# Low halves of the input projection's weights: stored in the second group of tokens instead of the first

## The chip, the cores and the metric

The kernel runs on one core of a Trainium2 chip. The metric is the device time of one execution in microseconds (us); lower is better. A core has five engines that run side by side, each working through its own list of instructions in order: TensorE (PE: matrix products; its weight loads are shown apart as PEld), VectorE (DVE), ScalarE (ACT), GpSimd (POOL) and SyncE (SP, which here issues nearly all DMA transfers). Engines wait for one another through semaphores. SBUF is the on-chip memory, PSUM the accumulators behind TensorE, and DRAM the chip's main memory.

## The reference

One decoder layer over 2048 tokens of width 1024, all in float32:

```
a = rmsnorm(x);  u = a @ W_in                      # 1024 -> 2560 columns
conv half:  glu = val * sigmoid(gate); causal depthwise conv of width 31; layernorm; silu
attention half: 8 heads of 64, stick-breaking attention
                A[t,s] = sigmoid(z_ts) * prod_{s<j<t} (1 - sigmoid(z_tj)), s < t;  then a head-wise rmsnorm
y = concat(conv, attn) @ W_out;  h = x + rmsnorm(y)
f = swiglu(rmsnorm(h)) with 2816 hidden columns;  out = h + rmsnorm(f)
```

## The kernel before

**Products in two halves.** TensorE multiplies in a reduced float32 format. To keep full precision, every operand X is split into a high half H, which is X rounded to that format by ScalarE, and a low half L = X - H. Each product is then three matmuls: L·H', H·H' and H·L'. For weights, ScalarE makes H (L554) and GpSimd makes L (L558); for activations, VectorE makes L.

**Groups.** The tokens are four groups of 512. The input projection (`inproj`, plan entry "in") runs once for each group. It goes through 20 weight blocks of 128 x 1024 (four each of gate, val, q, k, v), each of 512 KB in float32, and each takes 24 matmuls (`dense`; the lines L600, L602, L604 of the profile). The output projection (`outproj`, 8 tiles of weights) also runs for each group, and the first feed-forward products (`c11`, 22 tiles) for two of the groups.

**Weights.** `load_w` brings one weight tile. `Weights.next` calls it two blocks ahead of use; the tiles `raw`, `wH` and `wL` rotate through 2, 3 and 3 buffers. It loads the raw weights (L553) and makes H (L554). The first time that a tile is used it makes L (L558) and stores it to DRAM (L560) under the key of its source and number in the dictionary `kept`; at each later use it loads L from there (L556) and GpSimd does nothing. So of the 80 input-projection blocks, the 20 of group 0 are made and stored, and the 60 of groups 1 to 3 are loaded.

**What runs beside it.** The list `PLAN` sets the main stages. Three side streams are drawn along by the position in it: the attention (`attn_s`), the taps of the convolution (`taps_s`, on VectorE, L826) and sums of feed-forward weights (`sums_s`, on GpSimd, L1201). In the attention, a block of scores is turned into products by a scan on VectorE: for blocks on the diagonal L916 with the constant mask `lower` and the tile `om`, both in SBUF; for the others L918, one of whose operands is in PSUM. The result is transposed by TensorE (L936), split (ScalarE L592 makes TH, VectorE L593 makes TL) and multiplied with the values (L941, L942).

**Order.** All instructions up to the end of the mixing part (about 1420 us) are collected in a `Graph`. A list scheduler (`arrange`) with a cost for each kind of instruction, for transfers and for hops between engines simulates them, tries 13 orders, and keeps the shortest. `in_order` then pins each engine's order to it. The scheduler treats engines as independent of each other apart from data and buffers. SP's queue is ordered by it too; a DMA whose data or buffer isn't ready holds up the DMAs behind it. After that the rest of the feed-forward part (`five` and the down projection) runs in an order written out in the code.

Of the kernel before, what the change touches and what calls it, by code (L numbers as in the profile page):

```python
# [10 lines left out]
F32 = mybir.dt.float32  # L11
# [8 lines left out]
P = 128  # L20
S = 2048
D = 1024
# [459 lines left out]
def layer_kernel(ctx: ExitStack, tc: tile.TileContext, x, xT, g_pre_mix, w_in, conv_w, conv_b, ln_g, ln_b,  # L482
                 attn_g, w_out, g_post_mix, g_pre_ffn, w_gate, w_up, w_down, g_post_ffn, out):
    nc = tc.nc
    cp = ctx.enter_context(tc.tile_pool(name="consts", bufs=1))
    dp = ctx.enter_context(tc.tile_pool(name="scratch", bufs=1, space=DRAM))
# [57 lines left out]
    kept = {}  # L544

    def load_w(w):

        src, n = w
        H = wp.tile([P, D], F32R, tag="wH", name="wH", bufs=3)
        L = wp.tile([P, D], F32R, tag="wL", name="wL", bufs=3)  # L550
        key = id(src), n
        raw = wp.tile([P, D], F32, tag="raw", name="raw")
        nc.sync.dma_start(raw, src[n])  # L553
        nc.scalar.activation(H, raw, AF.Copy)  # L554
        if key in kept:
            nc.sync.dma_start(L.bitcast(F32), kept[key])  # L556
            return H, L
        nc.gpsimd.tensor_tensor(L, raw, H.bitcast(F32), ALU.subtract)  # L558
        kept[key] = dp.tile([P, D], F32, name=f"wL_{len(kept)}")
        nc.sync.dma_start(kept[key], L.bitcast(F32))  # L560
        return H, L

    def half_w(w):
# [10 lines left out]
    class Weights:  # L574


        def __init__(self, srcs, ahead=2, load=load_w):
            self.srcs = list(srcs)
            self.load = load
            self.tiles = []  # L580
            self.n = 0
            self.ahead = ahead
# [1222 lines left out]
```

## Time and profile before

| | us |
|---|---|
| Median of 3 runs | 2428.36 |
| Lowest and highest | 2428.14, 2428.55 |
| Profiled execution, its own time | 2429.93 |
| Span of the profiled execution | 2428.1 |

The span is the time from the first to the last instruction of the profiled execution. "Busy" is the time in which an engine executes at least one instruction. An idle stretch is put down to the event that ended it. In the views below a line such as L558 is a line of the kernel, "x20" a count, and "x<-y" a tile written from y. The DMA figures of the page are 656.67 MB moved in all, 270 GB/s on average. Among the queues, SP's carries 77.3% of the time of 16 DMA engines.

Of the low halves, the trace has 50 made and stored (20 of the input projection, 8 of the output projection, 22 of `c11`) and 106 loaded (60, 24 and 22).

### The profile page before, as it was taken

What the parts mean: (1) busy time and instruction counts of PE and PEld (TensorE: products, weight loads), DVE (VectorE), ACT (ScalarE), POOL (GpSimd) and SP (SyncE); (2) the same over time, 40 slices, a digit from 0 to 9 for tenths busy, and PEclk for the clock granted to TensorE, in tenths of its full rate; (3) what the DMA queues carried; (4) which work ended last, traced back from release to release, by engine and by line L of the source; (5) the groups of instructions that cost most, each with busy time, mean ns of one, the idle gap of its engine ahead of it and who ended that gap; (6) DMA issues with size and microseconds to landing.
All of it is one profiled execution on the core that took longest, in us unless ns stands there. A gap on an engine that the chain in (4) does not pass through costs nothing. (4 is left out here: it accounts for less than half of the span.)

```text
span 2428.1 us, 33643 instructions
## 1 busy us (share of the span) xinstructions
PE 2353.6 (97%) x11156; PEld 1929.4 (79%) x11156; DVE 1766.3 (73%) x2177; ACT 1163.8 (48%) x2078; POOL 1196.0 (49%) x994
## 2 busy tenths in 40 slices
PE   7999999999999999999999998999999999999998
PEld 5778888788888878887888877777888888887886
DVE  6897899999997799847832357667666664556557
ACT  4346555574555455455564553333232235454443
POOL 5462336422424333428700057755766665467656
PEclk9999999999999999999999999999999999999999
DMA  9888876998688899987897769878888877668765
GB/s 315 266 263 313 259 248 216 308 314 266 223 300 310 264 321 341 314 290 257 266 341 244 272 227 335 310 257 277 295 286 267 271 253 257 196 191 280 236 191 178
DMA packets 283790, 656.67 MB, mean 270 GB/s; under 512 B 34912, under 2 KB 35424, under 8 KB 283616
## 3 DMA queue, kind: packets, MB, share of 16 engines
q1 hardware_dynamic: 267776, 625.68, 77.3%
q10 hardware_dynamic: 15840, 28.84, 3.1%
q8 instruction: 88, 1.44, 0.2%
q14 instruction: 86, 0.70, 0.1%
HBM read 460.40 MB, written 193.99 MB: 270 GB/s over the span
## 5 line engine op out<-in xcount | busy, mean ns | idle before, releaser
L826 DVE SCALAR_TENSOR_TENSOR cv<-glu,cw,cv 128x512 f32<-128x512 f32 x464 | 346.9, 748 | 6.2
L1411 POOL TENSOR_TENSOR wL<-raw,wH 128x512 fp32r<-128x512 f32 x176 | 254.8, 1470 | 194.5 <-ACT wH L1410 163.1
L1642 DVE TENSOR_TENSOR xL__20078<-t__20080,xH__20077 128x512 fp32r<-128x512 f32 x154 | 200.4, 1306 | 159.9 <-ACT xH__20077 L1641 159.8
L1640 POOL TENSOR_TENSOR xL__20076<-t__20079,xH__20075 128x512 fp32r<-128x512 f32 x154 | 212.7, 1388 | 153.6 <-ACT xH__20075 L1639 145.4
L593 DVE TENSOR_TENSOR TL<-at,TH 128x512 fp32r<-128x512 f32 (+1 forms) x320 | 189.5, 601 | 127.7 <-ACT TH L592 117.3
L600 PE MATMUL inps<-xH,wL 128*128 128x512 f32 x640 | 259.4, 406 | 9.9 <-ACT sg L770 8.8
L604 PE MATMUL inps<-xL,wH 128*128 128x512 f32 x640 | 255.7, 401 | 0.6 <-DVE xL L740 0.6
L602 PE MATMUL inps<-xH,wH 128*128 128x512 f32 x640 | 256.3, 401 | 0.0
L1117 PE MATMUL dps<-xL__20076,xH__20077 128*128 128x512 f32 x616 | 240.1, 390 | 2.8 <-POOL xL__20076 L1640 2.8
L1117 PE MATMUL dps<-xH__20075,xL__20078 128*128 128x512 f32 x616 | 240.1, 390 | 2.5 <-DVE xL__20078 L1642 2.1
L1117 PE MATMUL dps<-xH__20075,xH__20077 128*128 128x512 f32 x616 | 239.8, 389 | 0.0
L554 ACT ACTIVATE wH<-raw 128x1024 fp32r<-128x1024 f32 x156 | 165.4, 1061 | 139.9 <-PE inps L604 62.9
L592 ACT ACTIVATE TH<-at 128x512 fp32r<-128x512 f32 (+1 forms) x320 | 168.8, 537 | 130.2 <-PE at L936 113.7
L913 ACT ACTIVATE om<-z 128x512 f32<-128x512 f32 (+2 forms) x320 | 168.8, 542 | 89.3 <-PE z L911 87.8
L1639 ACT ACTIVATE xH__20075<-t__20079 128x512 fp32r<-128x512 f32 x154 | 97.3, 632 | 217.2 <-POOL xL__20076 L1640 121.2
L558 POOL TENSOR_TENSOR wL<-raw,wH 128x1024 fp32r<-128x1024 f32 x50 | 123.1, 2467 | 155.9 <-ACT wH L554 119.3
L936 PE MATMUL at<-idr,om 128*128 128x128 f32 x1088 | 185.4, 273 | 7.2 <-DVE TL L593 2.7
L1410 ACT ACTIVATE wH<-raw 128x512 fp32r<-128x512 f32 x176 | 101.2, 623 | 167.7 <-PE b L1117 49.8
L936 PEld LDWEIGHTS at<-idr,om 128*128 128x128 f32 x1088 | 136.8, 140 | 48.0 <-DVE TL L593 6.3
L1201 POOL TENSOR_TENSOR sum<-sum 128x512 f32<-128x512 f32 x88 | 124.6, 1416 | 100.2 <-DMA sum<-in_w_up_dram 40.3
L918 DVE TENSOR_TENSOR_SCAN om<-om,z 128x512 f32<-128x512 f32 x124 | 156.8, 1271 | 8.5 <-ACT om L913 8.2
L600 PEld LDWEIGHTS inps<-xH,wL 128*128 128x128 f32 x640 | 121.7, 190 | 34.5 <-ACT sg L770 5.8
(296 smaller groups left out, 6103.9 us busy)
## 6 DMA issues: line engine op xcount, KB each, us to landing
wL<-wL SPq DMA_DIRECT2D x156, 512.0 KB, 5.3
raw<-in_w_in_dram SPq DMA_DIRECT2D x80, 512.0 KB, 5.8
t__20080<-u SPq DMA_DIRECT2D x154, 256.0 KB, 2.8
c<-c ACTq DMA_DIRECT2D x88, 256.0 KB, 5.3
t__20079<-wd SPq DMA_DIRECT2D x88, 256.0 KB, 2.9
K<-kd SPq DMA_DIRECT2D x80, 256.0 KB, 4.9
V<-vd SPq DMA_DIRECT2D x80, 256.0 KB, 5.0
u<-accf SPq DMA_DIRECT2D x22, 768.0 KB, 4.6
```

What stands on the lines that cost most here:

```text
L592: nc.scalar.activation(H, ps, AF.Copy)
L593: nc.vector.tensor_tensor(L, ps, H.bitcast(F32), ALU.subtract)
L600: nc.tensor.matmul(ps, WL[:, kc], aH[t](k), start=k == 0, stop=False)
L602: nc.tensor.matmul(ps, WH[:, kc], aH[t](k), start=False, stop=False)
L604: nc.tensor.matmul(ps, WH[:, kc], aL[t](k), start=False, stop=k == KT - 1)
L826: nc.vector.scalar_tensor_tensor(to, gl[c][:, k:k + G], cw[:, c, k:k + 1], a, ALU.mult, ALU.add)
L913: nc.scalar.activation(om[:, 0:w], z[:, 0:w], AF.Sigmoid, scale=-0.125)
L936: nc.tensor.transpose(pt[:, j * P:(j + 1) * P], u["A"][j][:, b * P:(b + 1) * P], id32)
L1117: return nc.tensor.matmul(ps, a, b, skip_group_check=True, **flags)
L1411: nc.gpsimd.tensor_tensor(l, t, f32(h), sub)
L1640: nc.gpsimd.tensor_tensor(WL, w, f32(WH), sub)
L1642: nc.vector.tensor_tensor(UL, t, f32(UH), sub)
```

## The change

For weights of the input projection (`src is w_in`) the first use makes the low half and returns without storing it; the key gets an empty tuple. The second use finds the empty tuple, makes the low half once more, allocates the DRAM tile and stores it. The third and fourth uses load it. Weights of other matrices are made and stored at the first use, as before. The value in the dictionary becomes a tuple with one tile. The name of a new DRAM tile is still taken from the number of keys in the dictionary, which doesn't grow between the second uses of the 20 blocks.

```diff
-        if key in kept:
-            nc.sync.dma_start(L.bitcast(F32), kept[key])
+        if kept.get(key):
+            nc.sync.dma_start(L.bitcast(F32), kept[key][0])
             return H, L
         nc.gpsimd.tensor_tensor(L, raw, H.bitcast(F32), ALU.subtract)
-        kept[key] = dp.tile([P, D], F32, name=f"wL_{len(kept)}")
-        nc.sync.dma_start(kept[key], L.bitcast(F32))
+        if src is w_in and key not in kept:
+            kept[key] = ()
+            return H, L
+        kept[key] = dp.tile([P, D], F32, name=f"wL_{len(kept)}"),
+        nc.sync.dma_start(kept[key][0], L.bitcast(F32))
         return H, L
```

Counted over the kernel: 20 more subtractions on GpSimd (70 for 50), 20 fewer loads of low halves (86 for 106), and as many stores (50), 20 of them later.

## The prediction

> **What bounds the kernel now.** I read the page first: the engine totals and the busy tenths in 40 slices.
>
> ```profile
> span 2428.1 us, 33643 instructions
> PE 2353.6 (97%) x11156; PEld 1929.4 (79%) x11156; DVE 1766.3 (73%) x2177; ACT 1163.8 (48%) x2078; POOL 1196.0 (49%) x994
> ...
> PE   7999999999999999999999998999999999999998
> ...
> DVE  6897899999997799847832357667666664556557
> ...
> DMA  9888876998688899987897769878888877668765
> ```
>
> TensorE is busy for 97% of the span, so the time can move only by what TensorE waits, and all its idle time is 2428.1 - 2353.6 = 74.5 us. The change touches no matmul. Behind TensorE the slices show VectorE nearly full through the first third, and DMA at eight or nine tenths but not full.
>
> Next I cut the span where the low halves are made and loaded: those of group 0 are made before 157 us (the view of L558 below), and group 1's stretch goes from there to about 360 us. This is the view by stretches; its columns are PE, PEld, DVE, ACT and POOL busy, the clock, the DMA share and GB/s.
>
> ```profile
> 0.00:157.00 157.00, 134.55 (x627) 108.62 (x628) 125.15 (x171) 65.54 (x112) 91.02 (x88) 0.98 0.89 282
> 157.00:360.00 203.00, 199.57 (x1060) 165.41 (x1058) 179.21 (x266) 119.56 (x222) 65.81 (x77) 1.00 0.84 273
> ...
> 157.00:200.00 43.00, 42.11 (x225) 35.38 (x224) 40.48 (x64) 26.39 (x51) 13.01 (x14) 1.00 0.89 301
> 200.00:280.00 80.00, 79.12 (x426) 65.38 (x424) 59.72 (x88) 49.38 (x92) 25.06 (x38) 1.00 0.90 296
> 280.00:360.00 80.00, 78.34 (x414) 64.66 (x412) 79.01 (x116) 43.80 (x80) 27.73 (x26) 1.00 0.76 235
> ```
>
> TensorE is idle 157 - 134.55 = 22.4 us in group 0 and 203 - 199.57 = 3.4 us in group 1. GpSimd is 58% busy in group 0 (91.02 of 157) and 32% in group 1 (65.81 of 203). VectorE has 20.3 us to spare between 200 and 280 us, and almost none at 280 to 360 us (79.01 of 80). Then I asked what TensorE waited for, first up to 157 us, then from 157 to 360 us (total us, times, longest).
>
> ```profile
> PE tps L610 <- DVE xrow L686: 11.0, 4, 7.3
> PE inps L600 <- ACT sg L770: 5.9, 2, 4.7
> PE at L936 <- DVE om L916: 2.1, 2, 1.3
> PE o L942 <- DVE TL L593: 1.5, 1, 1.5
> PE at L936 <- DVE TL L593: 1.1, 1, 1.1
> ...
> PE at L936 <- ACT ma L976: 0.9, 1, 0.9
> PE cps L853 <- DVE acc L847: 0.6, 1, 0.6
> PE z L910 <- DVE om L918: 0.5, 1, 0.5
> PE inps L600 <- DVE glu L775: 0.5, 1, 0.5
> ```
>
> No row names a DMA or a weight tile. In both groups TensorE waits for VectorE and ScalarE, and for weights never. In group 1 only some 2.5 us is there to be won at all.
>
> **The change part by part.** In group 0, `load_w` still makes the low half on GpSimd (L558) but no longer stores it. In group 1 it makes the low half again and stores it then. Groups 2 and 3 load it as now. So 20 stores move from group 0 to group 1, 20 loads of group 1 go, and 20 GpSimd subtractions come into group 1. The view of L558 by stretches and the list of DMA issues give the sizes:
>
> ```profile
> 0.00:157.00 157.00, 50.16 (x20) 0.98 0.89 282
> 157.00:360.00 203.00, 4.90 (x3) 1.00 0.84 273
> ...
> L558 POOL TENSOR_TENSOR wL<-raw,wH x50: 2344/2404/3321, 11.4 to 1036.9; 128x1024 fp32r<-128x1024 f32 x50
> ...
> wL<-wL SPq DMA_DIRECT2D x156, 512.0 KB, 5.3
> ```
>
> *Stores out of group 0.* 20 x 512 KB is 10.5 MB, about 37 us of transfer at that stretch's 282 GB/s. The gain is what TensorE waits for because of it. The one candidate is the 4.7 us wait for `sg` at 57 us, whose ScalarE predecessor carries a DMA as its releaser:
>
> ```profile
> 51.92 3.92 DVE L826 SCALAR_TENSOR_TENSOR cv<-glu,cw,cv 128x512 f32<-128x512 f32 x5
> ...
> 55.75 0.42 DVE L593 TENSOR_TENSOR vt<-vps,vt 128x256 fp32r<-128x256 f32 x1
> ...
> 56.20 0.38 ACT L592 ACTIVATE vt<-vps 128x256 fp32r<-128x256 f32 x1 [3.27 <-DMA QH<-qd]
> ```
>
> But the ScalarE copy starts at 56.20, at the end of the VectorE `vt` (55.75 + 0.42 = 56.17), and that one stood behind five taps that fill VectorE from 51.92. It is VectorE's backlog, and fewer stores don't shorten it. Bounds: 0, or -4.7 us if it was the DMA after all; I take 0, the nearer row.
>
> *Loads out of group 1.* The load's wait for a free buffer goes from SP's queue:
>
> ```profile
> SPq L556 <- PE inps L600: 25.4, 12, 4.1
> ```
>
> SP is then less held up, so what is queued behind it (K, V and Q for the attention, the next raw weights) starts earlier. TensorE waits for none of these in the rows above, so 0. The store that comes instead waits on SP for L558, as group 0's does today. SP issues as many DMAs as before in group 1 and 20 fewer in group 0. The DMA engines carry the same bytes in group 1, written instead of read.
>
> *Subtractions into group 1.* 20 x 2404 ns = 48.1 us. GpSimd goes to (65.81 + 48.1) / 203 = 56%, so it doesn't become the bound. The weight tile comes two blocks ahead, and a block takes 203 / 20 = 10.2 us; that hides ScalarE's rounding and the 2.4 us behind it. If that cover were gone, a late tile would stop TensorE for up to 2.4 us each. Small GpSimd steps that others wait for (`oT`, `pv`, `step`) can queue behind one. TensorE has two such waits up to 1420 us:
>
> ```profile
> PE pf L957 <- POOL oT L1014: 1.6, 1, 1.6
> ...
> PE vps L788 <- POOL step L782: 0.6, 1, 0.6
> ```
>
> I take 0, and as upper bound their sum once more, 2.2 us.
>
> What isn't hidden is VectorE. Here are the attention's diagonal scans (L916, both tensor inputs in SBUF) by stretches, the scan and the subtraction at 113 us, and the taps (one input in PSUM) up to 157 us and after it:
>
> ```profile
> 0.00:157.00 157.00, 25.11 (x21) 0.98 0.89 282
> 157.00:200.00 43.00, 9.79 (x11) 1.00 0.89 301
> 200.00:280.00 80.00, 11.03 (x12) 1.00 0.90 296
> 280.00:360.00 80.00, 11.11 (x12) 1.00 0.76 235
> ...
> 113.17 2.53 POOL L558 TENSOR_TENSOR wL<-raw,wH 128x1024 fp32r<-128x1024 f32 x1 [0.47 <-ACT wH L554]
> ...
> 114.01 2.77 DVE L916 TENSOR_TENSOR_SCAN om<-lower,om 128x512 f32<-128x512 f32 x1
> ...
> L826 DVE SCALAR_TENSOR_TENSOR cv<-glu,cw,cv 128x512 f32<-128x512 f32 x90 | 67.7, 752 | 2.2
> L826 DVE SCALAR_TENSOR_TENSOR cv<-glu,cw,cv 128x512 f32<-128x512 f32 x78 | 58.3, 747 | 0.5
> ...
> L1201 POOL TENSOR_TENSOR sum<-sum 128x512 f32<-128x512 f32 x12 | 15.9, 1328 | 16.8 <-DMA sum<-in_w_up_dram 11.0 <-issue 5.5
> ```
>
> A scan takes 25.11 / 21 = 1.196 us in group 0, with GpSimd 58% busy, and (9.79 + 11.03 + 11.11) / 35 = 0.912 us in group 1, with 32%: 0.284 us more for 26 points of GpSimd share, 0.0109 us a point. The scan that starts at 114.01, inside a subtraction that ends at 115.70, takes 2.77 us. The taps don't change (752 against 747 ns). So a VectorE instruction with two SBUF inputs stands still while GpSimd works.
>
> The Trainium skill ("SBUF — State Buffer", section "SBUF: two separate sides") states this as an exclusive lock: a VectorE instruction with two SBUF inputs and a GpSimd instruction that reads SBUF share a port pair, and whoever comes second "fully blocks" until the first has ended. The rows agree, the taps included. By the rule alone, with chance starts, each scan would meet one of the new subtractions with chance 48.1 / 203 = 0.24 and lose half of 2.4 us, an estimate of 0.28 us a scan, 10 us in all for VectorE; that belongs to the first rival below.
>
> My sum goes by the rows. The order of the mixing part is made by the kernel's own planner, which knows GpSimd's load but no such blocking; I let it move the 12 `sum` steps (15.9 us) out of group 1. That leaves 56% - 8% = 48%, 16 points more than now, 0.175 us a scan. The 12 scans between 200 and 280 us lie beside 20.3 us of idle VectorE; the other 23 cost 23 x 0.175 = 4.0 us where VectorE is full. In group 0 the same excess was 21 x 0.284 = 6.0 us, and TensorE's waits behind scans and `TL` were 2.1 + 1.5 + 1.1 = 4.7 us, 0.78 of it. So 4.0 x 0.78 = **3.1 us**. Bounds: 0 if VectorE's slack takes all, and 35 x 24 x 0.0109 = 9.2 us if no `sum` moves and all of it passes to TensorE.
>
> *The new plan.* The planner orders every instruction before about 1420 us anew. The trace of before can't show what that does. As bound I take the largest single row of TensorE's waits up to 1420 us that the change could make go, or bring once more:
>
> ```profile
> PE inps L600 <- ACT sg L770: 8.8, 4, 4.7
> ```
>
> That is 8.8 us either way; I take 0, since nothing says which.
>
> **Sum:** 0 + 0 + 0 + 3.1 + 0 = +3.1 us. The profiled execution took 2429.93 us, 1.8 us more than its span of 2428.1, and lies 1.57 us above the median of the runs, 2428.36. The span would become 2431.2, and the median 2428.36 + 3.1 = **2431.5 us**.
>
> **The rivals.**
> - *Slower.* VectorE's blocking isn't absorbed: the mechanism above at its upper end, 9.2 us, gives 2437.6; with the queueing on GpSimd, 2439.8. It decides once more than 4.9 us passes to TensorE, that is, once no `sum` leaves group 1 and the scans fall where VectorE is full. For it: 79.01 of 80 us of VectorE at 280 to 360 us, and every wait of TensorE naming VectorE or ScalarE. Against: 20.3 us of slack from 200 to 280 us. (By the estimate from the Trainium skill's page "SBUF — State Buffer", 10 us times 0.78, this would be 2436.)
> - *Faster.* The DMA relief or the shorter plan tells: the wait at 57 us goes (2423.7), or all `sg` waits (8.8 us, 2419.6). For it: the DMA engines are busy for 0.89 of group 0. Against: no wait of TensorE there names a DMA.
> - *The change doesn't do what it says.* All 20 stores of group 1 get a tensor of the same given name (the dictionary no longer grows). If they shared one place, stores would wait for the loads of groups 2 and 3. But the names in the DMA list carry a number of their own behind the given one, so I don't expect it:
>
> ```profile
> raw<-S_(5, 3)_5437 SPq DMA_DIRECT2D x2, 512.0 KB, 5.6
> ```
>
>   If it were so, the order of stores and loads couldn't hold, and the time would be well above 2440.
>
> **How the numbers follow.** Some 0.2% (4.9 us) is what a measurement of this kernel can tell from no change. The forecast, up to 4.9 us either way with its centre at +3.1: 0.5. Slower by blocking that isn't absorbed, or a worse plan: 0.28. Faster by relief or a better plan: 0.2. Not as described: 0.02, slower with it. So faster 0.2, same 0.5, slower 0.3. The range goes from 2428.4 - 8.8 = 2419.6 to 2439.8: 2420 to 2440. The cases that don't differ from no change lie in 2423.5 to 2433.2.
>
> **What would show it.** Right: 40 L558 instructions up to the end of group 1, 20 loads fewer, GpSimd near half busy in group 1, its L916 scans at about 1.1 us, and TensorE there with 3 us more of waits for `om` or `TL`. The `sg` wait in group 0 stays if it was VectorE's. Wrong: scans unchanged in group 1; TensorE's idle time in group 0 down by several us with DMA share; or differences after 430 us larger than those before, which would be the plan's doing.

## The result: 38 us slower

| | before, us | after, us |
|---|---|---|
| Median of the runs | 2428.45 | 2466.26 |
| Lowest and highest | 2428.14, 2429.96 | 2464.51, 2472.63 |
| Span of the profiled execution | 2428.1 | 2465.8 |

The ratio is 1.0162, with a 95% interval of 1.015 to 1.0174. The forecast was 2431.5 us in a range of 2420 to 2440: the direction of its centre was right, the size off by a factor of twelve.

First the page of the changed kernel, engine totals:

```profile
span 2465.8 us, 33652 instructions
PE 2365.5 (96%) x11156; PEld 1936.4 (79%) x11156; DVE 1810.5 (73%) x2177; ACT 1167.9 (47%) x2078; POOL 1241.6 (50%) x1014
```

TensorE runs the same 11156 instructions; VectorE the same 2177, but is busy for 1810.5 - 1766.3 = 44 us longer. Equal work with longer instructions means that they stand still while they run. GpSimd has its 20 instructions more and 1241.6 - 1196.0 = 45.6 us.

TensorE's row holds two parts of the loss. Its idle time goes from 2428.1 - 2353.6 = 74.5 us to 2465.8 - 2365.5 = 100.3 us, 25.8 us more. The other 11.9 us of the 37.7 us of span are a longer busy time for the same matmuls: the mean granted clock of the profiled execution is 0.989, against 0.995 before.

The view by stretches (PE, PEld, DVE, ACT and POOL busy, clock, DMA share, GB/s), the changed kernel first:

```profile
0.00:157.00 157.00, 132.50 (x601) 108.26 (x602) 127.21 (x163) 64.15 (x108) 94.36 (x89) 0.96 0.73 229
157.00:360.00 203.00, 192.40 (x995) 155.83 (x994) 180.31 (x242) 109.75 (x204) 116.13 (x98) 0.99 0.86 266
360.00:430.00 70.00, 57.90 (x294) 47.32 (x292) 66.26 (x76) 38.03 (x71) 38.70 (x28) 0.92 0.68 214
430.00:860.00 430.00, 418.12 (x2108) 344.33 (x2109) 394.35 (x538) 235.44 (x420) 156.78 (x185) 0.98 0.83 276
860.00:1420.00 560.00, 551.70 (x2722) 449.76 (x2721) 376.07 (x462) 303.84 (x527) 178.44 (x132) 1.00 0.83 281
```

and the rows of the kernel before that the prediction didn't show:

```profile
360.00:430.00 70.00, 68.37 (x338) 54.77 (x339) 69.01 (x93) 37.30 (x68) 43.20 (x31) 1.00 0.71 232
430.00:860.00 430.00, 423.37 (x2159) 349.29 (x2158) 394.65 (x539) 241.98 (x433) 156.45 (x182) 1.00 0.85 283
860.00:1420.00 560.00, 551.65 (x2703) 449.69 (x2702) 355.94 (x435) 302.62 (x525) 189.13 (x137) 1.00 0.86 295
```

TensorE's busy time in group 1 goes from 199.57 to 192.40 us and from 360 to 430 us from 68.37 to 57.90 us; from 860 to 1420 us nothing is lost. The clock is lower in every stretch up to 860 us. What TensorE waited for, up to 157 us, from 157 to 360 us, and from 360 to 462 us (total us, times, longest):

```profile
PE inps L603 <- ACT sg L773: 4.7, 1, 4.7
PE inps L603 <- DVE qkL L596: 4.5, 1, 4.5
PE at L939 <- DVE TL L596: 2.2, 1, 2.2
...
PE at L939 <- DVE TL L596: 4.7, 4, 1.7
...
PE at L939 <- DVE om L919: 1.2, 2, 0.9
...
PE at L939 <- DVE TL L596: 13.9, 1, 13.9
```

In group 1 the waits for `TL` and the scans' `om` are 5.9 us, where the kernel before had 0.5. One wait of 13.9 us stands out. This is the timeline around it, GpSimd's rows, then VectorE's (start, duration, instruction, count):

```profile
415.79 2.39 POOL L558 TENSOR_TENSOR wL<-raw,wH 128x1024 fp32r<-128x1024 f32 x1 [4.73 <-ACT wH L554]
418.20 1.68 POOL L1017 TENSOR_TENSOR oT<-oT,vsh 64x512 f32<-64x512 f32 x1
419.84 1.27 POOL L716 TENSOR_TENSOR xcol<-xcol,rb 128x512 f32<-128x512 f32 x1
421.08 2.34 POOL L558 TENSOR_TENSOR wL<-raw,wH 128x1024 fp32r<-128x1024 f32 x1
423.38 8.58 POOL L716 TENSOR_TENSOR xcol<-xcol,rb 128x512 f32<-128x512 f32 x7
431.92 1.26 POOL L1204 TENSOR_TENSOR sum<-sum 128x512 f32<-128x512 f32 x1
...
416.87 16.86 DVE L877 TENSOR_TENSOR xL<-ma,xH 128x512 fp32r<-128x512 f32 x2
433.65 0.68 DVE L596 TENSOR_TENSOR TL<-at,TH 128x512 fp32r<-128x512 f32 x1
```

Two subtractions on VectorE, 0.68 us each when free, take 16.86 us. The view of the tile `xL` in that window has them singly (shortest, median and longest in ns):

```profile
L877 DVE TENSOR_TENSOR xL<-ma,xH x2: 1866/8468/15069, 416.9 to 418.7; 128x512 fp32r<-128x512 f32 x2
```

The one from 416.9 takes 1.87 us and waits for the end of the first GpSimd instruction. The one from 418.7 takes 15.07 us and waits until the whole train of GpSimd instructions, that is, instructions following one another without a gap, has ended at 433.18. VectorE works in order, so everything behind it waits, `TL` first and TensorE for `TL`. A smaller one of the kind stands at 82 us:

```profile
81.40 1.30 POOL L1017 TENSOR_TENSOR oT<-oT,vsh 64x512 f32<-64x512 f32 x1 [2.29 <-ACT oT L1009]
82.66 4.73 POOL L558 TENSOR_TENSOR wL<-raw,wH 128x1024 fp32r<-128x1024 f32 x2
87.32 1.06 POOL L784 TENSOR_TENSOR step<-vs 128x511 f32<-128x511 f32 x1
...
81.88 7.58 DVE L919 TENSOR_TENSOR_SCAN om<-lower,om 128x512 f32<-128x512 f32 x1
```

The scan takes 1.27 us when free. Both blocks begin while `oT` is added on 64 partitions, for heads 0 and 6; even heads use the lower ones, 0 to 63. In every other case of the two traces a VectorE instruction was late by at most 2.2 us, one GpSimd instruction, also in the middle of a train.

The long wait costs more than itself. The same view by stretches around it:

```profile
410.00:420.00 10.00, 10.00 (x59) 8.43 (x58) 10.00 (x9) 8.32 (x15) 5.24 (x4) 1.00 0.40 118
420.00:434.00 14.00, 0.45 (x2) 0.01 (x1) 14.00 (x2) 0.60 (x1) 13.17 (x10) 0.59 0.47 143
434.00:438.00 4.00, 3.62 (x12) 3.14 (x13) 3.49 (x6) 0.99 (x2) 0.00 (x0) 0.50 0.00 0
438.00:442.00 4.00, 4.00 (x19) 3.34 (x19) 2.95 (x5) 1.37 (x3) 0.00 (x0) 0.79 0.01 2
```

TensorE's granted clock is 0.50 in the 4 us after the wait and 0.79 in the next 4, some 2.8 us of full speed lost.

For the sections below, *excess* is the sum, over VectorE's instructions, of the duration less that of an undisturbed one of the same tiles and shape (the tenth percentile in the kernel before).

### The profile page after: what moved, and what is told of

The parts are those of the page before. It is cut to its first block, busy times and chain, and to the rows that moved or that the text cites. A ratio compares the mean times of both kernels' runs of the same rounds, so it can differ in the third digit from the quotient of the medians.

```text
span 2465.8 us, 33652 instructions
## 1 busy us (share of the span) xinstructions
PE 2365.5 (96%) x11156; PEld 1936.4 (79%) x11156; DVE 1810.5 (73%) x2177; ACT 1167.9 (47%) x2078; POOL 1241.6 (50%) x1014
## 5 line engine op out<-in xcount | busy, mean ns | idle before, releaser
L558 POOL TENSOR_TENSOR wL<-raw,wH 128x1024 fp32r<-128x1024 f32 x70 | 171.0, 2448 | 213.3 <-ACT wH L554 196.2
L919 DVE TENSOR_TENSOR_SCAN om<-lower,om 128x512 f32<-128x512 f32 (+3 forms) x128 | 148.9, 1183 | 17.9 <-ACT om L916 17.6
```

## The experiments

### The same order, one instruction wider or narrower

The planner's costs know the columns of an instruction, not its partitions. So the addition to `oT` can be widened and all engines keep the changed kernel's order, instruction by instruction.

`after_full`:

```diff
-                nc.gpsimd.tensor_tensor(oT[hp, :], oT[hp, :], vsh[hp, :], ALU.add)
+                nc.gpsimd.tensor_tensor(oT, oT, vsh, ALU.add)
```

> The changed kernel in the same order on every engine; only the GpSimd addition to oT (L1017) covers all 128 partitions instead of 64, in the same time. It adds the other head's rows to the other half too, so the attention's numbers differ. Theory A (a GpSimd instruction on half of the partitions lets those queued behind it keep the port, so a VectorE instruction with two SBUF inputs waits out the whole train): the 7.6 us scan at 82 us and the 15.1 us subtraction at 419 us fall to under 3 us each, TensorE's 13.9 us wait goes, and the time falls by 15 to 22 us, to about 2447. Rival B (any train of back-to-back GpSimd instructions does that): nothing changes, 2466. Rival C (the new order itself is bad, whatever the port does): 2466.

Measured: 2441.97 us, 1.0058 of the kernel before (1.004 to 1.0075), so 24.3 us less than the changed kernel. In its timeline:

```profile
82.56 1.87 DVE L919 TENSOR_TENSOR_SCAN om<-lower,om 128x512 f32<-128x512 f32 x1
...
409.51 3.58 DVE L877 TENSOR_TENSOR xL<-ma,xH 128x512 fp32r<-128x512 f32 x2
```

The scan takes 1.87 for 7.58 us, the pair of subtractions 3.58 for 16.86. Theory A holds, with 2 us more than the 15 to 22 it gave, and B and C fall for this part. VectorE's two blocks were 6.3 + 14.4 = 20.7 us of excess; 24.3 us go, which fits with the lost clock on top.

`after_top`, the same line with the upper 64 partitions always:

```diff
-                nc.gpsimd.tensor_tensor(oT[hp, :], oT[hp, :], vsh[hp, :], ALU.add)
+                nc.gpsimd.tensor_tensor(oT[DH:P, :], oT[DH:P, :], vsh[DH:P, :], ALU.add)
```

> The changed kernel in the same order on every engine, and the GpSimd addition to oT stays on 64 partitions, but always on the upper 64 (for even heads it takes the other head's rows, so the attention's numbers differ). Theory A as the small measurement refined it (only an instruction that leaves out the last partitions lets the train behind it keep the port): no VectorE instruction is held over several GpSimd instructions, and the time is that of after_full, 2438 to 2447. Rival (half the partitions is what counts): 2460 to 2470.

Measured: 2444.06 us, 1.0068 (1.0049 to 1.0086). The order is the changed kernel's, the instruction as short in partitions, and the blocks are gone. It is the lower half that does it, not the half.

`before_full`, the first edit on the kernel before:

> The kernel before with the same one edit (128 partitions instead of 64, other numbers in the attention). Theory A: no VectorE instruction was held for longer than one GpSimd instruction in it, so the time stays, 2425 to 2431. Rival: a wider addition is better or worse by itself, a change of over 5 us.

Measured: 2428.78 us in one run. As far as one run tells, a wider addition is neither better nor worse by itself.

### The port by itself

`micro_port`, in place of the layer, for each case (its first addition on partitions `q`):

```
nc.gpsimd.tensor_tensor(o[0][q, :], seed[q, :], b[q, :], ALU.add)
for k in range(n): nc.gpsimd.tensor_tensor(o[k + 1], b, b, ALU.add)
nc.vector.tensor_tensor(d[0], ps, seed, ALU.add)
nc.vector.tensor_tensor(d[1], ps if where == "psum" else b, seed, ALU.subtract)
```

> Not the layer: x is copied to the output, and beside it nine cases run three times each. In a case GpSimd adds once on 32, 64 or 128 partitions and then 0 to 8 times on 128, back to back; VectorE first adds with an input in PSUM and then subtracts with two SBUF inputs (or one in PSUM) while the first addition runs. Theory A: after a 128-partition start the subtraction waits for that one addition, about 1.3 us at most; after a 64-partition start it waits for the whole train, 8 x 1.25 = 10 us, 5 us behind 4, 2.5 us behind 2; with an input in PSUM it waits for nothing. Rival B: 10 us after both starts. Rival E (one instruction at most, always): under 1.5 us everywhere.

VectorE's subtractions of one round, in order of time. The cases shown are: partitions 0 to 63 with 8 additions behind, all 128 with 8, 64 to 127 with 8, 0 to 63 with 4, with 2, with none, with 8 and an input in PSUM; last, 0 to 31 with 8:

```profile
169.24 8.28 DVE L41 TENSOR_TENSOR half_d<-b,quart_s 128x512 f32<-128x512 f32 x1
180.37 1.32 DVE L41 TENSOR_TENSOR full_d<-b,half_s 128x512 f32<-128x512 f32 x1
191.52 1.31 DVE L41 TENSOR_TENSOR half_d<-b,full_s 128x512 f32<-128x512 f32 x1
202.66 4.23 DVE L41 TENSOR_TENSOR half0b_d<-b,half_s 128x512 f32<-128x512 f32 x1
209.75 2.31 DVE L41 TENSOR_TENSOR half0c_d<-b,half0b_s 128x512 f32<-128x512 f32 x1
214.91 1.31 DVE L41 TENSOR_TENSOR half0d_d<-b,half0c_s 128x512 f32<-128x512 f32 x1
218.91 0.68 DVE L41 TENSOR_TENSOR half0p_d<-ps,half0d_s 128x512 f32<-128x512 f32 x1
...
240.30 8.28 DVE L41 TENSOR_TENSOR quart_d<-b,fullp_s 128x512 f32<-128x512 f32 x1
```

and GpSimd's instructions of the first of these cases:

```profile
168.74 1.25 POOL L37 TENSOR_TENSOR half_g<-quart_s,b 64x512 f32<-64x512 f32 x1 [1.46 <-ACT quart_s L45]
...
169.96 8.45 POOL L39 TENSOR_TENSOR half_g<-b 128x512 f32<-128x512 f32 x8
```

Behind a start on the lower partitions the subtraction grows with the train: 1.31, 2.31, 4.23, 8.28 us for 0, 2, 4, 8 additions behind. The first two add 1.0 us together, each further one 1.0 us. It ends at 177.52, 0.9 us before the train (178.41), so here it gets through just before the end. Behind a full start, or one on the upper half, it takes 1.3 us, one instruction. With an input in PSUM there is no wait (0.68 us). So theory A holds, at 0.83 to 0.92 of its sizes, and B and E fall; what A had wrong is that any half does it: the third row shows 1.31 us.

The Trainium skill ("SBUF — State Buffer", "SBUF: two separate sides") has the loser of the port pair blocked for the whole of the other's instruction. The full starts agree; the lower-half starts don't: there the hold spans instructions, and the measurement decides. Another page of the Trainium skill ("GPSIMD Engine Reference", "2.1 Instruction dispatch") says that GpSimd's eight cores, each with 16 partitions, go on to the next instruction without waiting for each other. Cores without a share that run ahead would fit the lower-half rows, but by itself this doesn't explain the third, where cores have no share either; no run here shows a core by itself.

### The added subtractions by themselves

`after_full_set`: as `after_full`, and still the same order; the 20 low halves of group 1 are written with zeros. The planner is given the subtraction's cost and reads for them.

```diff
-        nc.gpsimd.tensor_tensor(L, raw, H.bitcast(F32), ALU.subtract)
+        (group 1 of w_in) nc.gpsimd.memset(L.bitcast(F32), 0.0)    # planned as the subtraction
```

> As after_full, again in the same order, but the 20 low halves of group 1 are set to zero (a write only, no read of SBUF) instead of being subtracted, so that the products with them are left out in value. Theory A with single collisions for the rest: VectorE's excess from 180 to 375 us (19 us in the changed kernel, 9 before) goes back to 9 to 12, and the time falls by another 5 to 9 us against after_full, to about 2440. Rival B/C: the subtractions' own price is nothing, the same time as after_full. Rival D (the added subtractions are the whole loss): 2430.

Measured: 2435.68 us, 1.0028 (1.0013 to 1.0043), 6.3 us less than `after_full`. The diagonal scans between 157 and 360 us, in the kernel before, the changed kernel, `after_full` and `after_full_set`:

```profile
157.00:360.00 203.00, 31.94 (x35) 1.00 0.84 273
```

```profile
157.00:360.00 203.00, 44.72 (x37) 0.99 0.86 266
```

```profile
157.00:360.00 203.00, 42.58 (x36) 0.99 0.85 267
```

```profile
157.00:360.00 203.00, 35.00 (x36) 0.99 0.85 270
```

A scan takes 0.91, 1.21, 1.18 and 0.97 us. With zeros in place of the subtractions it is near the old price, and 6.3 us of time go with it, though the two sets of runs overlap (2439 to 2449 us and 2432 to 2442 us). TensorE's busy time in this stretch (the first number after the length) is in `after_full` and `after_full_set`:

```profile
157.00:360.00 203.00, 193.93 (x1002) 156.96 (x1003) 180.08 (x242) 110.97 (x205) 111.22 (x96) 0.99 0.85 267
...
157.00:360.00 203.00, 198.14 (x1029) 162.05 (x1027) 176.63 (x250) 115.64 (x214) 84.72 (x96) 0.99 0.85 270
```

That is the term that the prediction had priced at 3.1 us, the single collisions. A write of zeros is also shorter, 0.95 us where a subtraction takes 2.48 us, so these runs don't part the missing reads from the shorter GpSimd time. The excess from 180 to 375 us falls from 18.6 to 11.8 us, into the expected 9 to 12. What is left, 2435.68 - 2428.45 = 7.2 us, is in neither, and its cause stays open.

### Other orders of the same instructions

One constant of the planner's model is moved; the instructions stay.

```diff
-RATE, ISSUE, AHEAD, LAND = 350.0, 450.0, 700.0, 5000.0
+RATE, ISSUE, AHEAD, LAND = 350.0, 450.0, 650.0, 5000.0
```

> The changed kernel with one constant of the planner's model moved (AHEAD from 700 to 650 ns), nothing else: another order of the same instructions. Theory A with chance (the long blocks are a matter of which instructions meet): the blocks fall elsewhere or are absent, and the time is 2440 plus 0 to 25 us, with the excess over 2440 found in blocks behind the lower-half additions. Rival (the change costs 38 us in any order): 2460 to 2472.

> The kernel before with the same constant moved. Theory A with chance: blocks can occur here too; without one 2423 to 2435, with one up to 2450. Rival (the order matters little, the kernel before is safe from blocks): 2425 to 2432.

and with 600, 680 and 720:

> The kernel before, AHEAD at 600 ns: one more order of the same instructions. Theory O (the order's luck is most of the loss, and the order of the kernel before is a good one): 2430 to 2455. Rival S (the change costs over 25 us in any order): 2425 to 2437.

> The changed kernel, AHEAD at 600 ns. Theory O: 2438 to 2465, overlapping with the orders of the kernel before, their means 5 to 15 us apart, and a long block behind a lower-half addition where it is over 2455. Rival S: over 2455 always.

> The kernel before, AHEAD at 680 ns. Theory O: 2430 to 2455. Rival S: 2425 to 2437.

> The changed kernel, AHEAD at 680 ns. Theory O: 2438 to 2465. Rival S: over 2455.

> The kernel before, AHEAD at 720 ns. Theory O (the order's luck is most of the loss): 2430 to 2455. Rival S (the change costs over 25 us in any order): 2425 to 2437.

> The changed kernel, AHEAD at 720 ns. Theory O: 2438 to 2465. Rival S: over 2455.

Measured, in us (700 is the kernels themselves, the others one run each, where runs of one kernel can lie 9 us apart, as in `after_full`; blocks are single instructions of VectorE with an excess over 2.5 us up to 1420 us):

| AHEAD | before | after | difference | blocks, before | blocks, after |
|---|---|---|---|---|---|
| 700 | 2428.45 | 2466.26 | 37.8 | none | 6.3, 14.4 |
| 650 | 2435.26 | 2455.74 | 20.5 | none | 3.7 |
| 680 | 2441.42 | 2459.12 | 17.7 | none | none |
| 600 | 2449.65 | 2464.16 | 14.5 | 4.7 | 2.9, 12.9 |
| 720 | 2451.23 | 2463.24 | 12.0 | 3.9 | 12.4 |

The first pair already misses: `after_650` lies in theory A's range, but its one block of 3.7 us doesn't make the 16 us over 2440, and `before_650` is just over its 2435. Neither of the later theories is met as put: O has the sets overlap with means 5 to 15 us apart, S a difference over 25 us. They don't overlap, and the four new pairs differ by 12.0 to 20.5 us, 16.2 in the mean. The order alone moves the kernel before by up to 23 us, and its own order is the best of the five, 16 us under the mean of the other four (2444.4). The changed kernel's own is 5.7 us over the mean of its other four (2460.6). So of the 37.8 us, 16.2 are what the change costs in the mean of these four orders, 15.9 are the good order that it gives up, and 5.7 an order worse than most. The causes found above and this reckoning cut the same 38 us in two ways; they don't add.

The blocks of 12 to 14 us in three of the five orders of the changed kernel are all the same meeting, between 406 and 419 us: `xL<-ma`, while GpSimd works through `oT`, `wL` and the eight `xcol` of group 2. None of the five orders before has it. All eight blocks of the table stand in a train of GpSimd instructions that has an even head's addition to `oT` in it, on the lower half; no odd head's addition has a block behind it. But the loss doesn't need blocks: `after_680` has none and is 17.7 us over its pair.

The excess in group 1 (180 to 375 us) is 12.0 to 20.2 us in the orders after and 4.8 to 9.3 us before: that part comes with the change in all five orders. Up to 1420 us the pairs differ in excess by 33.7, 25.7, 16.5, 21.9 and 7.6 us, in the order of the table. The four new pairs have 17.9 us of excess for 16.2 us of time in the mean, which fits VectorE's waiting as the price of the change; no run shows it. Between orders of one kernel it doesn't fit: the kernel before has 77.9 us of excess in its own order, the fastest, and 72.9 us at 680.

### Trying to mend it

`after_lock`, `before_lock`: the planner doesn't start a VectorE instruction with two SBUF inputs while GpSimd reads SBUF, nor the other way round.

```diff
+            wide = sum(place(a) == "SB" and width(a) > 1 for a in ins)
+            o.lock = not dma and (eng == "Pool" and wide > 0 or eng == "DVE" and wide > 1)
...
+                    if o.lock and lock[OTHER[e]] > t + 1e-9:
+                        held.append((prio[n], n))
+                        heapq.heappush(ev, (lock[OTHER[e]], 1, n, ()))
+                        continue
```

> The changed kernel with a planner that knows the port: a VectorE instruction with two SBUF inputs isn't started while GpSimd reads SBUF, nor the other way round; the planner fills VectorE with others meanwhile. Theory A: VectorE's excess before 900 us falls (80 us in the changed kernel, 42 of it before 375 us); the blocks behind lower-half additions can remain; 2425 to 2445. Rival (the excess isn't what TensorE waits for): 2460 or more.

> The kernel before with the planner that knows the port. Theory A: VectorE's excess up to 900 us (50 us) falls and the time with it, 2415 to 2428, if the plan's times hold on the chip; as in the changed kernel with this planner the excess may fall little (82 for 112 us there, most of it the long block), then 2428 to 2440.

Measured: 2451.81 us (1.0095, 1.0079 to 1.0111) and 2454.86 us (1.01, 1.0082 to 1.0118). The changed kernel gains 14 us, the kernel before loses 26, though its excess up to 900 us didn't rise (46.5 us against 49.6). Both miss their ranges, and each still has a block behind head 0's addition, of 4.5 and 4.1 us at 89 us. So the excess isn't all that decides; where in TensorE's order it falls may be the rest, which no run isolates.

`before_upper`, `after_upper_680`, `before_upper_lock`: the correction is loaded head by head into the upper half, so that no GpSimd addition leaves out the upper partitions.

```diff
-                hp = slice(h % 2 * DH, (h % 2 + 1) * DH)
-                nc.gpsimd.tensor_tensor(oT[hp, :], oT[hp, :], vsh[hp, :], ALU.add)
+                nc.sync.dma_start(vsh[top, n:G], vsd[h // 2][hp, g * G + n:(g + 1) * G])
+                nc.gpsimd.tensor_tensor(oT[top, :], oT[top, :], vsh[top, :], ALU.add)
```

> The kernel before, with the addition to oT on the upper 64 partitions for every head (the correction may go to either half, since the two are summed later; it is loaded head by head, 32 transfers of 128 KB for 16 of 256 KB), and so a new order. Theory A: the kernel before loses nothing to long blocks, so only the order's own spread is seen, 2421 to 2436. Rival: the kernel before pays for lower-half additions too, under 2421.

> The changed kernel with the same edit, results as the reference's, and AHEAD at 680 ns in the planner's model, so a new order again. Theory A: no long block can occur, and what is left is the added subtractions' single collisions and the order's spread, 2433 to 2450, below the changed kernel's 2466. Rival (the 38 us are the change's in any order): 2460 or more.

> Both edits on the kernel before. Theory A: as before_lock but with no long block possible, 2415 to 2432. Rival (order's spread decides): anything from 2421 to 2440, with no relation to the excess.

Measured: 2445.93 us (1.0066, 1.0051 to 1.0081), 2461.22 us (1.0132, 1.0116 to 1.0148) and 2461.85 us (1.0133, 1.0118 to 1.0148). All three miss theory A upwards; the second lies where its rival put it (2460 or more), the third above its rival's range too. No long block is in them, and yet they are no faster than other orders of their kernels: 2446 lies among the before's five, 2461 among the after's, and 2462, like `before_lock`, above all five of the kernel before. With new orders the blocks' absence is worth less than the order's spread. No version beat the kernel before.

## Why the prediction was wrong

- **What bounds the kernel: right about the waits.** TensorE waits for VectorE and ScalarE, not for weights or DMA, before and after. **"So the time can move only by what TensorE waits" was wrong**: of the 37.7 us, 11.9 are a longer busy time for the same matmuls, at a lower granted clock. The sum has no term for it.
- **Stores out of group 0, worth 0: right.** The DMA share there fell from 0.89 to 0.73, and the wait of 4.7 us for `sg` at 57 us stayed as it was: VectorE's backlog, as read from the timeline. In `after_full` TensorE is busy for 135.76 us of this stretch, 1.2 us more than before; whether the stores or the order did that isn't shown.
- **Loads out of group 1, worth 0: right as far as seen.** No wait of TensorE names a K, V or Q.
- **Subtractions into group 1, 3.1 us: mechanism right, mis-sized by half.** The same-order experiment gives 6.3 us, and TensorE's waits for `TL` and `om` there grew by 5.4 us where "3 us more" was the sign named. I let the planner move the `sum` steps out of group 1; it left 15 there, and GpSimd came to 116.13 / 203 = 57%, the upper case. The scans rose by 0.30 us each (44.72 / 37 against 0.91), where 0.175 was taken and 0.26 was the bound.
- **"Bounds: ... 9.2 us if no `sum` moves and all of it passes to TensorE": this step failed.** It priced VectorE's waits by the averages of groups 0 and 1, 0.0109 us a point of GpSimd's share, and in these no wait is longer than one GpSimd instruction. The runs show 6.3 and 14.4 us of excess in single instructions behind lower-half additions, 24.3 us of time in the changed kernel's order. The trace of before has no such case, and it does have VectorE passing through the middle of a train, so the bound was read off a sample that lacked the event. Only a measurement of its own could have given the price.
- **"The new plan ... I take 0", with 8.8 us either way: this step failed too.** Four other orders of the kernel before are 7 to 23 us slower, none faster. A bound taken from one row of waits is no bound on a new order: the order at hand was the best of the five tried.
- **The rivals.** *Slower* by VectorE's blocking or a worse plan, at 0.28, had the right direction and two of the causes, at too small a price (2437.6 to 2439.8). *Faster* by DMA relief didn't happen. The change did what it said: 19 L558 steps before 157 us and 22 in the next stretch. No view shows whether each store has a tensor of its own; SP's loads of low halves waited 4.2 us in all for another transfer of a low half, against 0.6 before, and `after_full` has the same stores and is 24.3 us faster.

## What to carry to other kernels

Where a planner or a scheduler fixes the order of everything, an edit is priced together with a new order: run a few orders of both versions before calling an edit of half a per cent good or bad. A VectorE instruction with two SBUF inputs pays for GpSimd's work beside it, and in these runs the place of that work counted for more than its amount. A GpSimd instruction that leaves out the upper partitions, followed by others without a gap, can stop such an instruction for nearly the whole train, as here for 15.07 us.

## What the hardware showed that was not expected

- After a GpSimd addition on partitions 0 to 63 or 0 to 31, VectorE's subtraction took 8.28 us with 8 further additions behind, and 1.31 us after one on 64 to 127 or 1.32 us on all 128. Why the lower half differs is open. It is also open when the hold ends early: in the kernel before a subtraction at 404.6 us was late by only 1.1 us in a train that began with a lower-half addition. And the block of 3.9 us at AHEAD 720 began 11 us after the lower-half addition of its train had ended, with full additions in between.
- After 14 us of idle time TensorE's granted clock was 0.50 for 4 us and 0.79 for the next 4.
